# Feed-forward products by one level of Strassen's block algorithm, in a two-layer fp32 encoder on one core

## The chip, the core and the metric

The kernel runs as one launch on one core of a Trainium2 chip. The metric is device time in microseconds (us); the time of a version is the median of its runs. The core's engines are TensorE (PE in the profile; its weight loads are PEld), VectorE (DVE), ScalarE (ACT), GpSimd (POOL) and SyncE (SP). In this kernel SP issues all DMAs, in one queue.

## What is computed

One sequence of 1024 tokens of width 1024 goes through two layers. Layer 0 mixes by windowed attention, layer 1 by a gated linear scan (HGRN2); then each has a feed-forward stage and a gated addition of a projected side input p (called PLE in the kernel). All inputs are fp32. Cut to what matters:

```
def swiglu(x, w_in, w_out):            # w_in 1024 x 5632, w_out 2816 x 1024
    gu = x @ w_in
    g, u = jnp.split(gu, 2, axis=-1)
    return (jax.nn.silu(g) * u) @ w_out

for i in range(2):
    mix = windowed_gqa(x, ...) if i == 0 else hgrn2_bidirectional(x, ...)
    x = layer_norm(ALPHA * x + mix, ln_mix_g[i], ln_mix_b[i])
    x = layer_norm(ALPHA * x + swiglu(x, ffn_w_in[i], ffn_w_out[i]), ln_ffn_g[i], ln_ffn_b[i])
    x = x + jax.nn.sigmoid(x @ ple_w_gate[i]) * (p[i] @ ple_w_proj[i])
```

## The kernel before

**Tiles.** Everything is held transposed: 128 features in the partitions, 512 tokens (half of them, h = 0 or 1) in the free dimension. x is 8 such tiles for each half (index k or m), the hidden width 2816 is 22 tiles (index f). Activations live in the pool `acts` of 48 tiles of 128x512 fp32.

**Products.** An fp32 operand is split into a high part, which ScalarE makes by a copy that rounds to the type fp32r, and a low part, which VectorE or GpSimd makes by subtraction (`split`, lines 67 to 69). One product is three matmuls into the same PSUM bank, high by high, high by low and low by high (`mm3`, lines 182 to 185), each 128x128 by 128x512. `lin` is a chain of eight of these over k. Weights come raw from DRAM in tiles of 128x512 or smaller (`load_w`), through three buffers, and are split into five others; a list of all weight tiles in order of use (`plan`) is fetched one entry ahead of the products (`take_w`).

**Feed-forward stage** (`ffn_ple`). The 22 tiles f go in four groups of 5, 5, 6 and 6 (`GROUPS`). For each f and h, `pair` makes g and u (two `lin`, 24 matmuls each), silu and the product on ScalarE and VectorE, and splits the result h into the pool `hp` of 16 tiles. After each group `acc` multiplies its h tiles with `w_out` into one bank for each of 8 output tiles m and each half (fo), and adds the bank to the tile Y[m][h], which stays in `acts`.

**Normalization.** `layer_norm` is a generator that runs beside other products. Means over the features are taken on TensorE with a matrix of 1/1024 (`average`): first the mean (mu), then the sum of squares v of the eight tiles less the mean, its mean (var), square root and reciprocal (rs), then each tile times rs, with gain and bias on ScalarE, and its split into the new x (`new_x`, low parts on GpSimd).

**Order.** `weave(main, side, ratio)` advances a side generator by `ratio` steps for each step of the main one; the order of calls is the order of priority, from which a scheduler makes the order on each engine. In the feed-forward stage:

```
weave(first(0), pend, 0.65)
drain(first(1))
...
drain(last(0))
weave(last(1), norms[0], 0.9)
weave(ple(0), norms[1], 0.7)
```

`pend` is the normalization of the second half behind the mixer. Beside it stand the products of the first group for the first half (`first(0)`), which read only the first half of x. The output products of the last group go half by half (`last`), so that the normalization of the first half, `norms[0]`, stands beside those of the second, and `norms[1]` beside the PLE products of the first half.

## Time and profile before

| | |
|---|---|
| median of 3 runs | 2974.35 us (2973.11 to 2977.14) |
| span of the profiled execution | 2974.4 us |
| TensorE busy | 2846.8 us, 96% |
| VectorE, ScalarE, GpSimd busy | 58%, 37%, 23% |
| DMA | 197.22 MB, mean 66 GB/s |
| feed-forward matmuls | 6336 of 13584 |

The profile is one execution on the chip. "Busy" is the time in which at least one instruction of an engine runs; matmuls are pipelined and overlap, so the mean duration of one is not what it costs. Windows of the trace count instructions by their start. PEclk is the clock that TensorE was granted, as a share of full speed.

### The profile page before, as it was taken

The page shows a single profiled execution, that of the slowest core. Times are in us where ns is not written, and L with a number is a line of the kernel's source. Part 1 is how long each engine was busy: PE and PEld are TensorE (multiplying, and loading weights), DVE is VectorE, ACT ScalarE, POOL GpSimd, SP SyncE. Part 2 cuts the span into 40 slices and gives each one's busy share as a digit, 9 for nine tenths or more (in the row PEclk, how much of TensorE's full clock was granted, in tenths as well). Part 3 has the DMA queues.
Part 4 walks back from the last instruction along what each step waited for, and adds up shares of the span by engine and source line. Part 5 has one row for each costly group of instructions (what it writes and reads, how often), then busy time and mean ns, then how long its engine had stood idle before and what let it go on. Part 6 is the DMA issues. An engine that isn't in the chain of part 4 may idle for free.

```text
span 2974.4 us, 36435 instructions
## 1 busy us (share of the span) xinstructions
PE 2846.8 (96%) x13584; PEld 2319.0 (78%) x13584; DVE 1730.6 (58%) x2797; ACT 1100.1 (37%) x2032; POOL 678.5 (23%) x476
## 2 busy tenths in 40 slices
PE   8989999999999998999998999999999999999989
PEld 6666778888888886787887778778788888888867
DVE  6878886322223237758888887897843232222484
ACT  4555655221121225544444444344531212112362
POOL 4243242000000004653343433422400000000252
PEclk9999999999999999999999999999999999999999
DMA  4111233211111112321111211212221111111223
GB/s 159 48 43 47 68 98 94 61 54 39 57 42 55 46 57 78 100 85 64 58 64 54 65 50 54 67 54 82 86 90 56 38 55 50 45 48 54 75 96 117
DMA packets 117394, 197.22 MB, mean 66 GB/s; under 512 B 13536, under 2 KB 38880, under 8 KB 117216
## 3 DMA queue, kind: packets, MB, share of 16 engines
q1 hardware_dynamic: 117216, 194.88, 21.0%
q8 instruction: 107, 1.75, 0.2%
q14 instruction: 71, 0.58, 0.1%
HBM read 190.64 MB, written 4.19 MB: 66 GB/s over the span
## 4 chain that ended last, share of the span: by engine, by line
PE 76%; DVE 16%; ACT 4%; issue 3%; POOL 1%; DMA 1%; SPq 0%; DVEq 0%; ACTq 0%; POOLq 0%
PE u L185 5%; PE u L183 5%; PE u L184 5%; PE g L183 5%; PE g L184 5%; PE g L185 5%; PE fo L185 5%; PE fo L183 5%; PE fo L184 5%; PE zps L185 2%; PE zps L183 2%; PE zps L184 2%; PE lv L715 2%; PE s L360 2%; PE pgps L185 1%
## 5 line engine op out<-in xcount | busy, mean ns | idle before, releaser
L183 PE MATMUL fo<-h,w_fo 128*128 128x512 f32 x704 | 278.1, 395 | 0.0
L185 PE MATMUL fo<-h,w_fo 128*128 128x512 f32 x704 | 278.1, 395 | 0.0
L184 PE MATMUL fo<-h,w_fo 128*128 128x512 f32 x704 | 278.0, 395 | 0.0
L184 PE MATMUL g<-xl,w_fg 128*128 128x512 f32 x704 | 274.2, 390 | 3.2 <-POOL xl L69 3.1
L512 DVE TENSOR_TENSOR sg<-sg,u 128x512 f32<-128x512 f32 x88 | 60.5, 688 | 370.8 <-PE u L185 369.4
L183 PE MATMUL g<-xh,w_fg 128*128 128x512 f32 x704 | 274.3, 390 | 1.2 <-ACT sg L511 1.2
L185 PE MATMUL u<-xh,w_fu 128*128 128x512 f32 x704 | 274.6, 390 | 0.0
L183 PE MATMUL u<-xh,w_fu 128*128 128x512 f32 x704 | 274.6, 390 | 0.0
L184 PE MATMUL u<-xl,w_fu 128*128 128x512 f32 x704 | 274.4, 390 | 0.0
L185 PE MATMUL g<-xh,w_fg 128*128 128x512 f32 x704 | 274.0, 389 | 0.0
L69 POOL TENSOR_TENSOR w_hz<-r_hz,w_hz 128x512 fp32r<-128x512 f32 x128 | 181.1, 1422 | 330.5 <-ACT w_hz L68 322.9
L183 PE MATMUL zps<-xh_n,w_hz 128*128 128x512 f32 x512 | 213.4, 417 | 0.0
L68 ACT CAST w_fo<-r_fo 128x384 fp32r<-128x384 f32 (+1 forms) x160 | 78.6, 492 | 338.0 <-PE fo L185 276.2
L185 PE MATMUL zps<-xh_n,w_hz 128*128 128x512 f32 x512 | 203.6, 398 | 0.0
L184 PE MATMUL zps<-xl_n,w_hz 128*128 128x512 f32 x512 | 202.0, 394 | 0.0
L69 DVE TENSOR_TENSOR w_fu<-r_fu,w_fu 128x512 fp32r<-128x512 f32 x108 | 79.9, 742 | 161.4 <-ACT w_fu L68 161.4
L69 DVE TENSOR_TENSOR w_fo<-r_fo,w_fo 128x384 fp32r<-128x384 f32 (+1 forms) x160 | 88.3, 552 | 120.5 <-ACT w_fo L68 120.5
L185 PEld LDWEIGHTS fo<-h,w_fo 128*128 128x128 f32 x704 | 131.9, 187 | 32.3
L184 PEld LDWEIGHTS g<-xl,w_fg 128*128 128x128 f32 x704 | 132.3, 188 | 31.9 <-POOL xl L69 4.5
L184 PEld LDWEIGHTS fo<-h,w_fo 128*128 128x128 f32 x704 | 131.9, 187 | 32.3
L183 PEld LDWEIGHTS fo<-h,w_fo 128*128 128x128 f32 x704 | 132.0, 187 | 32.1
L222 POOL TENSOR_TENSOR s<-hy,hy 128x512 f32<-128x512 f32 x4 | 5.8, 1450 | 658.9 <-DVE hy L531 613.4
(291 smaller groups left out, 6836.2 us busy)
## 6 DMA issues: line engine op xcount, KB each, us to landing
r_hz<-in_whg_dram SPq DMA_DIRECT2D x128, 256.0 KB, 2.6
r_fg<-in_wfi_dram SPq DMA_DIRECT2D x108, 256.0 KB, 2.6
r_fu<-in_wfi_dram SPq DMA_DIRECT2D x108, 256.0 KB, 2.7
r_fo<-in_wfo_dram SPq DMA_DIRECT2D x128, 192.0 KB, 2.3
r_pg<-in_wpg_dram SPq DMA_DIRECT2D x64, 256.0 KB, 2.8
r_qkv<-in_wqkv_dram SPq DMA_DIRECT2D x40, 256.0 KB, 2.7
r_ao<-in_watt_o_dram SPq DMA_DIRECT2D x32, 256.0 KB, 2.7
r_hv<-in_wvh_dram SPq DMA_DIRECT2D x32, 256.0 KB, 3.0
```

The lines of the kernel that those rows point to most:

```text
L68: act.copy(hi, src)
L69: (eng or dve).tensor_tensor(lo, src, f32(hi), op=ALU.subtract)
L183: pe.matmul(ps, lhsT=w[0], rhs=x[0], start=start, stop=False)
L184: pe.matmul(ps, lhsT=w[0], rhs=x[1], start=False, stop=False)
L185: pe.matmul(ps, lhsT=w[1], rhs=x[0], start=False, stop=stop)
L222: (eng or dve).tensor_tensor(s, yprev, y, op=ALU.add)
L360: pe.matmul(sp[r][:, :n * P], lhsT=qq[rs], rhs=kk[rs], start=i == 0, stop=i == 2)
L512: dve.tensor_tensor(sg, sg, u, op=ALU.mult)
L715: pe.matmul(lv[:, c], lhsT=ks[:, c * P:(c + 1) * P], rhs=view(Qq, c * P, dims), start=True, stop=True)
```

## The change

The feed-forward products of both layers are made by one level of the Winograd form of Strassen's algorithm: a product of 2x2 blocks by seven block products of sums and differences, where before there were eight.

- **Input side.** The blocks of x are the feature halves (k 0 to 3 and 4 to 7) by the token halves; those of the weights are the two halves of the features for g and for u. For each f there are seven products p of four `mm3` (`times`): 1 and 2 read x of the first half as it is, 6, 5, 7 and 4 read the sums t2, t1, t3, t4 of x, and 3 reads x of the second half. Weight sums are made on GpSimd (in `head`, `both`, `mid_tail` of the plan), three or four for each f, and g and u come out by additions on VectorE. The order is 1 and 2 of f (`head`), 4 and 3 of f - 1 (`tail`), 6, 5 and 7 of f (`mid`).
- **Sums of x.** `layer_norm` of the second half behind the mixer now takes the tiles in the order 0, 4, 1, 5, ... and calls `combine` after every second one, which makes t1 to t4 (two on VectorE, two on GpSimd) and splits them and the second half of x, the four sums into the pool `hp` (tile `xc`).
- **What stands beside that normalization.** `all_early`: products 1 and 2 of the first four f (`NA`), in place of the first group's products for the first half; the ratio is 2.
- **DRAM.** `combine` stores the 16 tiles Y in DRAM. The h tiles are combined for pairs of f (`spill`, four differences on GpSimd for each pair) and the seven tiles of a pair are stored in DRAM; so are the sums of `w_out` (`w_sums`, four on GpSimd for each pair). One layer stores 77 + 44 + 16 tiles of 256 KB.
- **Output side** (`matmuls_out`). Blocks are the parity of f in a pair (11 pairs), the halves of the output features and of the tokens. It loads the 16 Y again, then runs seven products one after the other in the order 1, 2, 6, 7, 4, 5, 3, each of 11 steps; a step loads one tile of weights and one of h, splits both and runs 12 matmuls, into four banks. The low part of weights is made by GpSimd (VectorE for product 7), that of h by VectorE. After product 4 the first half is complete, and its normalization is woven beside products 5 and 3.
- **Weights** are fetched up to four entries ahead (three on the output side), and loads of three entries are begun ahead of their splits; raw tiles lie in `acts`. `w_out` is laid out by rows on the host.

The diff, cut to its core:

```diff
-GROUPS = [(0, 5), (5, 10), (10, 16), (16, 22)]
+AHEAD = 4
+NA = 4
+ORDER = [1, 2, 6, 7, 4, 5, 3]
...
+        def combine(Y, k):
+            a, b, c, d = Y[k][0], Y[k][1], Y[k + KH][0], Y[k + KH][1]
...
+            dve.tensor_tensor(t1, b, a, op=ALU.subtract)
+            dve.tensor_tensor(t2, d, t1, op=ALU.subtract)
+            pool.tensor_tensor(t3, d, b, op=ALU.subtract)
+            pool.tensor_tensor(t4, c, t2, op=ALU.subtract)
+            fx["x"][6].append(keep(t2, dve))
+            fx["x"][5].append(keep(t1, dve))
+            fx["x"][7].append(keep(t3, dve))
+            yield
+            fx["x"][4].append(keep(t4, pool))
+            hi, lo = A("xh22", F32R), A("xl22", F32R)
+            split(hi, lo, d, dve)
+            fx["x"][3].append((hi, lo))
+            for m in (k, k + KH):
+                for h in range(2):
+                    sync.dma_start(fx["y"][m, h], Y[m][h])
...
-            for m in range(KT):
+            mixed = which == 0 and h == 1
+            for m in [m + i for m in range(KH) for i in (0, KH)] if mixed else range(KT):
                 dve.tensor_tensor(ys[m], ys[m], rs, op=ALU.mult)
...
+                elif m >= KH:
+                    yield from combine(Y, m - KH)
...
+                def times(ps, f, p, start):
+                    w = take_w("w", f, p, ahead=AHEAD)
+                    for k in range(KH):
+                        mm3(ps, w[k], xs[p][k], start and k == 0, k == KH - 1, True)
...
+                def spill(k, sa, sb):
+                    (a, b), (c, d) = sa["h"], sb["h"]
+                    t3, t2, t4 = A("th3"), A("th2"), A("th4")
+                    pool.tensor_tensor(t3, d, b, op=ALU.subtract)
+                    pool.tensor_tensor(b, b, a, op=ALU.subtract)
+                    pool.tensor_tensor(t2, d, b, op=ALU.subtract)
+                    pool.tensor_tensor(t4, c, t2, op=ALU.subtract)
...
+                def matmuls_in():
+                    sts = {}
+                    for f in range(FT):
+                        st = sts[f] = {}
+                        if f >= NA:
+                            yield from head(f, st)
+                        if f:
+                            yield from tail(f - 1, sts[f - 1])
+                        store()
+                        yield from mid(f, st)
+                        if f % 2 == 0 and f:
+                            spill(f // 2 - 1, sts.pop(f - 2), sts.pop(f - 1))
+                        elif f % 2:
+                            w_sums(f // 2)
...
+                def matmuls_out():
...
+                            sync.dma_start(Y[m][h], fx["y"][m, h])
...
+                    for p in ORDER:
...
+                        for k in range(FP):
+                            w, hh = take_w("o", p, k, ahead=AHEAD - 1)
+                            for i in range(4):
+                                mm3(into[i], w[i], hh, p in (1, 2, 5) and k == 0, k == FP - 1, True)
...
-                weave(first(0), pend, 0.65)
-                drain(first(1))
...
-                weave(last(1), norms[0], 0.9)
+                weave(all_early(), pend, 2)
+                drain(matmuls_in())
+                out = matmuls_out()
+                while next(out) != "half":
+                    pass
+                weave(out, norms[0], 0.9)
                 weave(ple(0), norms[1], 0.7)
```

In two places the prediction rests on the order on an engine. The first is the start of the stage of layer 0. On TensorE before, where the output projection of attention (aops) is followed by the products of the first f:

```order
L184 MATMUL aops<-ql_2099,w_ao_4_4248 128x512
L185 MATMUL aops<-qh_2098,w_ao_4_4248 128x512
L183 MATMUL g<-xh_4215,w_fg_0_4300 128x512
L184 MATMUL g<-xl_4216,w_fg_0_4300 128x512
L185 MATMUL g<-xh_4215,w_fg_0_4300 128x512
```

TensorE after, where product 2 of the fourth early f (za) ends; xc are the split sums of x, and the first bank x behind za is product 6 of f 0:

```order
L318 MATMUL za<-xh_4348,w_4627 128x512
L319 MATMUL za<-xl_4349,w_4627 128x512
L320 MATMUL za<-xh_4348,w_4627 128x512
L318 MATMUL x<-xc,wp_4679 128x512
L319 MATMUL x<-xc,wp_4679 128x512
L320 MATMUL x<-xc,wp_4679 128x512
L318 MATMUL x<-xc,wp_4679 128x512
L319 MATMUL x<-xc,wp_4679 128x512
L320 MATMUL x<-xc,wp_4679 128x512
L318 MATMUL zy<-xc,wp_4729 128x512
```

Between the last product that reads only the first half of x and the first that reads a sum stand no other matmuls. VectorE before, from the reciprocal of the second half's normalization on (w_fg, w_fu are split weights, sg the gated product):

```order
L254 RECIPROCAL rs<-rs 128x256 x2
L512 TENSOR_TENSOR sg<-sg,u 128x512
L257 TENSOR_TENSOR y_3982<-y_3982,rs 128x512
L69 TENSOR_TENSOR w_fu_0_4648<-r_fu_0_4646,w_fu_0_4648 128x512
L69 TENSOR_TENSOR h_4643<-sg,h_4643 128x512
L69 TENSOR_TENSOR w_fu_4_4653<-r_fu_4_4651,w_fu_4_4653 128x512
L69 TENSOR_TENSOR w_fg_0_4658<-r_fg_0_4656,w_fg_0_4658 128x512
L257 TENSOR_TENSOR y_4038<-y_4038,rs 128x512
```

And after, from the same place (wp are split weights, tx the sums of x):

```order
L415 RECIPROCAL rs<-rs 128x256 x2
L74 TENSOR_TENSOR wp_4843<-wraw,wp_4843 128x512
L419 TENSOR_TENSOR y_3984<-y_3984,rs 128x512
L419 TENSOR_TENSOR y_4187<-y_4187,rs 128x512
L419 TENSOR_TENSOR y_4040<-y_4040,rs 128x512
L376 TENSOR_TENSOR tx_4657<-y_3984,y_2800 128x512
L419 TENSOR_TENSOR y_4239<-y_4239,rs 128x512
L377 TENSOR_TENSOR tx_4658<-y_4187,tx_4657 128x512
L419 TENSOR_TENSOR y_4091<-y_4091,rs 128x512
L696 TENSOR_TENSOR g_4674<-u_4624,za 128x512
L74 TENSOR_TENSOR xc<-tx_4658,xc 128x512
L74 TENSOR_TENSOR xc<-tx_4657,xc 128x512
```

The sums and their splits now stand among the eight multiplies by rs. GpSimd in the same place before:

```order
L224 TENSOR_TENSOR s<-s,y_4294 128x512
L69 TENSOR_TENSOR xl_4336<-y_3903,xh_4335 128x512
L69 TENSOR_TENSOR xl_4348<-y_3942,xh_4347 128x512
L245 TENSOR_TENSOR v<-v,sq 128x512 x4
L69 TENSOR_TENSOR xl_4637<-y_3982,xh_4636 128x512
```

And after (s and wraw are weight sums of the first f):

```order
L74 TENSOR_TENSOR xl_4349<-y_3944,xh_4348 128x512
L359 TENSOR_TENSOR s<-s,y_4300 128x512
L220 TENSOR_TENSOR s_4596<-wraw 128x512
L406 TENSOR_TENSOR v<-v,sq 128x512
L222 TENSOR_TENSOR s_4598<-wraw 128x512
L223 TENSOR_TENSOR wraw<-s_4598,wraw 128x512
L195 TENSOR_TENSOR wraw<-wraw 128x512
L406 TENSOR_TENSOR v<-v,sq 128x512 x3
L378 TENSOR_TENSOR tx_4659<-y_4187,y_3984 128x512
L379 TENSOR_TENSOR tx_4660<-y_3702,tx_4658 128x512
L74 TENSOR_TENSOR xc<-tx_4660,xc 128x512
```

Four weight sums now stand among the additions to v. The second place is where the input side of layer 0 ends, on SP. Before, at the end of the fourth group's output products, only weight loads stand in the queue:

```order
L74 DMA r_fo_0_7626<-in_wfo_dram 128x384
L74 DMA r_fo_3_7631<-in_wfo_dram 128x384
L74 DMA r_fo_0_7676<-in_wfo_dram 128x384
L74 DMA r_fo_3_7681<-in_wfo_dram 128x384
L74 DMA r_fg_0_7726<-in_wfi_dram 128x512
L74 DMA r_fg_4_7731<-in_wfi_dram 128x512
```

After, between the input and the output side (h_10 are the DRAM tiles of the last pair, th its differences; y the tiles Y that come back):

```order
L766 DMA h_10_4445<-h_7939 128x512
L766 DMA h_10_4412<-th_8087 128x512
L766 DMA h_10_4434<-th_8088 128x512
L794 DMA y_8100<-y_4364 128x512
L794 DMA y_8102<-y_4366 128x512
...
L794 DMA y_8114<-y_4378 128x512
L146 DMA wraw<-in_wfo_dram 128x512
L146 DMA wraw<-h_6_4386 128x512
```

The stores of the last pair stand ahead of the 16 loads of Y, and these ahead of the loads of output step 6.

## Rows read from the trace of the kernel before

**Rows 1.** Page, parts 1 and 2: span, engines, bandwidth in 40 slices.
```profile
span 2974.4 us, 36435 instructions
...
PE 2846.8 (96%) x13584; PEld 2319.0 (78%) x13584; DVE 1730.6 (58%) x2797; ACT 1100.1 (37%) x2032; POOL 678.5 (23%) x476
...
GB/s 159 48 43 47 68 98 94 61 54 39 57 42 55 46 57 78 100 85 64 58 64 54 65 50 54 67 54 82 86 90 56 38 55 50 45 48 54 75 96 117
```

**Rows 2.** Page, part 4: chain that ended last, shares by engine.
```profile
PE 76%; DVE 16%; ACT 4%; issue 3%; POOL 1%; DMA 1%; SPq 0%; DVEq 0%; ACTq 0%; POOLq 0%
```

**Rows 3.** Window: length, busy us of PE, PEld, DVE, ACT, POOL, clock, DMA, GB/s.
```profile
500.00:600.00 100.00, 100.00 (x436) 81.47 (x435) 35.29 (x57) 22.33 (x41) 0.00 (x0) 1.00 0.23 70
```

**Rows 4.** Page, part 5; tiles g, fo: ns shortest/median/longest, first and last start.
```profile
L184 PE MATMUL g<-xl,w_fg 128*128 128x512 f32 x704 | 274.2, 390 | 3.2 <-POOL xl L69 3.1
...
L183 PE MATMUL g<-xh,w_fg x704: 388/389/500, 430.5 to 2763.6; 128*128 128x512 f32 x176
...
L185 PE MATMUL fo<-h,w_fo x704: 392/396/397, 545.8 to 2838.1; 128*128 128x512 f32 x176
```

**Rows 5.** Timeline of PE, from u to fo: start, length, instruction.
```profile
1089.10 0.39 PE L183 MATMUL u<-xh,w_fu 128*128 128x512 f32 x1
...
1094.54 0.40 PE L183 MATMUL fo<-h,w_fo 128*128 128x512 f32 x1
...
1098.05 0.40 PE L183 MATMUL fo<-h,w_fo 128*128 128x512 f32 x1
```

**Rows 6.** Groups by line: busy us, mean ns, idle before.
```profile
L69 POOL TENSOR_TENSOR w_hz<-r_hz,w_hz 128x512 fp32r<-128x512 f32 x128 | 181.1, 1422 | 330.5 <-ACT w_hz L68 322.9 <-PE lv L715 4.6 <-issue 2.0
...
L69 DVE TENSOR_TENSOR w_fu<-r_fu,w_fu 128x512 fp32r<-128x512 f32 x108 | 79.9, 742 | 161.4 <-ACT w_fu L68 161.4
...
L68 ACT CAST w_fu<-r_fu 128x512 fp32r<-128x512 f32 x108 | 66.7, 618 | 102.4 <-PE fo L185 37.3 <-PE u L185 36.2 <-issue 21.2
...
L252 ACT ACT_TABLE_LOAD x7 | 9.0, 1283 | 0.1
```

**Rows 7.** Timelines of DVE, then POOL, second half's normalization, layer 0.
```profile
441.67 1.88 DVE L239 TENSOR_TENSOR y<-y,mu 128x512 f32<-128x512 f32 x3 [0.52 <-PE mu L230]
...
456.17 0.69 DVE L69 TENSOR_TENSOR avl<-v,avh 128x512 fp32r<-128x512 f32 x1
...
466.04 3.37 DVE L254 RECIPROCAL rs<-rs 128x256 f32<-128x256 f32 x2 [4.01 <-ACT rs L252]
...
474.06 2.48 DVE L257 TENSOR_TENSOR y<-y,rs 128x512 f32<-128x512 f32 x4
477.07 5.19 DVE L257 TENSOR_TENSOR y<-y,rs 128x512 f32<-128x512 f32 x3
...
454.18 1.30 POOL L245 TENSOR_TENSOR v<-v,sq 128x512 f32<-128x512 f32 x1 [1.29 <-DVE v L245]
...
478.63 6.17 POOL L69 TENSOR_TENSOR xl<-y,xh 128x512 fp32r<-128x512 f32 x4 [0.33 <-ACT xh L68]
```

**Rows 8.** Windows of 4 us, first half's normalization, layer 0; columns of Rows 3.
```profile
1160.00:1164.00 4.00, 4.00 (x18) 2.90 (x16) 4.00 (x5) 2.96 (x5) 4.00 (x3) 1.00 0.33 98
1164.00:1168.00 4.00, 0.03 (x1) 0.00 (x0) 4.00 (x3) 3.28 (x6) 4.00 (x4) 0.92 0.00 0
1168.00:1172.00 4.00, 1.22 (x2) 0.50 (x2) 4.00 (x5) 2.25 (x5) 4.00 (x3) 0.50 0.22 66
1172.00:1176.00 4.00, 2.50 (x6) 2.01 (x7) 4.00 (x5) 1.66 (x4) 2.58 (x2) 0.50 0.21 66
1176.00:1180.00 4.00, 4.00 (x16) 3.18 (x15) 1.37 (x3) 1.90 (x2) 0.00 (x0) 0.80 0.52 163
```

**Rows 9.** Window at the start; DMA issues, page part 6: KB, us to landing.
```profile
10.00:15.00 5.00, 5.00 (x15) 3.97 (x16) 3.95 (x7) 3.88 (x7) 0.94 (x1) 1.00 1.01 372
...
r_fg<-in_wfi_dram SPq DMA_DIRECT2D x108, 256.0 KB, 2.6
...
xraw<-in_xT_dram SPq DMA_DIRECT2D x16, 256.0 KB, 5.8
```

More of the change, by code (lines that the diff above doesn't have):

```diff
@@ L114, in take_w, with pair_of, blocks @@
             assert k == key, (k, key)
-            fetch_w()
-            return w
+            while len(ready) < ahead and at[0] < len(plan) and (not ready or plan[at[0]][3]):
+                fetch_w()
+            return w
+        fx = {}
+        def pair_of(raw, name, eng=None):
+            hl = wp.tile([P, 2, HALF], F32R, tag="hl", bufs=5, name=name)
+            split(hl[:, 0], hl[:, 1], raw, eng)
+            return hl[:, 0], hl[:, 1]
+        def blocks(hl):
+            return [(hl[0][:, k * P:(k + 1) * P], hl[1][:, k * P:(k + 1) * P]) for k in range(4)]
@@ L525, in acc @@
                         if k % 2:
                             yield
-                    y = Y[m][h]
-                    if gi == 0:
-                        dve.scalar_tensor_tensor(y, y, ALPHA, ps, ALU.mult, ALU.add)
-                    else:
-                        dve.tensor_tensor(y, y, ps, op=ALU.add)
-                    if st is not None:
-                        sum_in(st, y, m, Y[m - 1][h], pool)
-                def first(h):
-                    for f in range(*GROUPS[0]):
-                        yield from pair(f, [h], *w_in(f))
@@ L539, in last, with early @@
-                def last(h):
-                    gi = len(GROUPS) - 1
-                    f0, f1 = GROUPS[gi]
-                    s = T("to", "s")
-                    for m in range(KT):
-                        yield from acc(gi, m, h, take_w("fo", m), s)
-                    norms[h] = layer_norm([Y[m][h] for m in range(KT)], s, li, 1, X, h)
+                def early(f):
+                    x = bank("xa")
+                    yield from times(x, f, 1, True)
+                    u1 = u1s[f] = A("u1")
+                    act.copy(u1, x)
+                    z = bank("za")
+                    yield from times(z, f, 2, True)
+                    g0s[f] = g0 = A("g0")
+                    dve.tensor_tensor(g0, u1, z, op=ALU.add)
+                    act.activation(g0, g0, AF.Silu)
@@ new lines, in head, with mid, out @@
+                def head(f, st):
+                    x = st["x"] = bank("x")
+                    yield from times(x, f, 1, True)
+                    u1 = T("t0", "u1")
+                    act.copy(u1, x)
+                    z = MM("z")
+                    yield from times(z, f, 2, True)
+                    g0 = st["g0"] = A("g0")
+                    dve.tensor_tensor(g0, u1, z, op=ALU.add)
+                def mid(f, st):
+                    u1 = u1s.get(f)
+                    x = st["x"] = bank("x") if u1 is not None else st["x"]
+                    yield from times(x, f, 6, u1 is not None)
+                    u2 = st["u2"] = T("t1", "u2")
+                    def out(t):
+                        if u1 is None:
+                            act.copy(t, x)
+                        else:
+                            dve.tensor_tensor(t, u1, x, op=ALU.add)
+                    out(u2)
+                    z = st["z"] = bank("zy")
+                    yield from times(z, f, 5, True)
+                    yield from times(x, f, 7, False)
+                    u3 = st["u3"] = T("t2", "u3")
+                    out(u3)
+                    dve.tensor_tensor(u3, u3, z, op=ALU.add)
@@ new lines, in w_sums, with store @@
+                def w_sums(k):
+                    e, o = wfo[li][2 * k], wfo[li][2 * k + 1]
+                    a, b, c, d = get(e[:, :HALF]), get(o[:, :HALF]), get(e[:, HALF:]), get(o[:, HALF:])
+                    s3, s1, s2, s4 = sums(a, b, c, d)
+                    lag.append([(fx["sums"][p, k], t) for p, t in ((7, s3), (5, s1), (6, s2), (3, s4))])
+                def store(n=0):
+                    while len(lag) > n:
+                        for dst, src in lag.pop(0):
+                            sync.dma_start(dst, src)
@@ new lines, in matmuls_in @@
+                def matmuls_in():
+                    sts = {}
+                    for f in range(FT):
+                        st = sts[f] = {}
+                        if f >= NA:
+                            yield from head(f, st)
+                        if f:
+                            yield from tail(f - 1, sts[f - 1])
[5 more added lines that the diff above has]
+                            w_sums(f // 2)
+                    yield from tail(FT - 1, sts[FT - 1])
+                    store()
+                    spill(FP - 1, sts[FT - 2], sts[FT - 1])
+                    store()
```

273 lines of the change are left out of this document (218 added, 55 removed).

## The prediction

> **What bounds the kernel now.** I read the page's first two parts [rows 1], then its chain [rows 2], then a window of 100 us inside a feed-forward stage [rows 3]. TensorE is busy 96% of the span and the chain runs through it for 76%; in the stage that the change rewrites it is busy 100.00 of 100.00 us at full clock, while VectorE has 35 us of work and GpSimd none. So this stage costs what its matmuls cost, and there is room on every other engine. A matmul's mean duration there, 389 to 396 ns [rows 4], is not its cost, since they overlap: 24 of the u matmuls start from 1089.10 on and the fo matmuls follow them at 1094.54, so they stand 0.227 us apart; the first 16 of the fo matmuls start between 1094.54 and 1098.05, 0.234 us apart [rows 5]. The u matmuls read tokens from the pool `acts`, the fo matmuls from `hp`; this is the only difference that I see, and I let the spacing go by the pool. Feed-forward matmuls are 704 in each of nine groups [rows 4], 6336 in all, 3168 a layer: 2112 at 0.227 and 1056 at 0.234 make 726 us of a layer, 1452 us of the span.
>
> All sums below are made against the profiled execution, whose span of 2974.4 us [rows 1] is the median of the runs within 0.1 us.
>
> **Part 1: fewer matmuls.** Seven block products take the place of eight. Per layer the input side goes from 2112 to 22 x 7 x 12 = 1848, the output side from 1056 to 7 x 11 x 12 = 924; 792 fewer in the program, as its order shows on TensorE (12150 rows, then 11358). Of the input products three of seven (1, 2, 3) read `acts` and four `hp`: 792 x 0.227 + 1056 x 0.234 = 426 us; output 924 x 0.234 = 216 us. Together 642, a gain of **84 us a layer**. If all input products ran at 0.227 it would be 91, if all ran at 0.234, 78.
>
> **Part 2: the element work beside them.** Per f the input side has 84 matmuls, 19.4 us. GpSimd gets 8 operations for it (4 weight sums, and half of 8 for a pair of f), VectorE 12, ScalarE 12. By prices of the same shapes [rows 6] that is 8 x 1.42 = 11.4, 12 x 0.74 = 8.9 and 12 x 0.62 = 7.4 us. Each fits alone. VectorE and GpSimd slow each other: three multiplies took 5.19 us (1.73 each) beside four GpSimd operations in 6.17 (1.54 each), where alone they took 0.62 and 1.30 [rows 7]. Pairing all 8 at 1.73 and the other 4 VectorE operations at 0.74 gives 16.8 us, still under 19.4. The output side has 2.8 us for each step of 12 matmuls, with one GpSimd operation, one of VectorE and two of ScalarE: 1.73 at most, and 1.24. So I take the element work of the steady loops at nothing, hidden under the matmuls; what it costs without that cover is a rival below.
>
> **Part 3: transfers.** A step of the output side loads two tiles of 0.262 MB in 2.8 us, 187 GB/s; the input side moves 23 tiles for two f, 155 GB/s. The trace of before never needs so much here, but at its start it moved 372 GB/s over 5 us [rows 9]. I take the steady transfers at nothing too.
>
> **Part 4: the seam into the feed-forward products.** Before, the normalization of the second token half runs beside the first group's products, which want only the first half. Now only products 1 and 2 of four f are free of the second half: 96 matmuls, 21.8 us. Product 6 then wants t2 of all four blocks, which come last out of that normalization. In layer 0 (times of before): first product 430.5 [rows 4]; 3.1 us of waits for its split pieces [rows 4]; 21.8; five or six us for the averages and for products 6 and 5 of f 0. Unhindered TensorE would be through these at 462. The data: the first subtraction of the mean is at 441.67 and the variance was summed when the split of `avl` came at 456.17 [rows 7]. GpSimd now has four weight sums among its four additions to v, but VectorE has fewer splits in its way; I leave it at 456. Then two splits, two matmuls, a table load of 1.28, the root, reciprocals 3.37 [rows 6, 7], some 8 us with hand-overs: 464 (466 to 470 before, where the variance matmul stood later among others). From there VectorE has 32 operations up to the last piece of t2, beside 12 on GpSimd: 12 pairs at 1.73 and 20 at 0.62 make 33; I take 31, since the first ones run before GpSimd starts. So 495, and TensorE loses 495 - 462 = 33 us. After a wait the clock also stays low: after that at 1164 it was granted 0.50 from 1168 to 1176, the lower of its two levels, 1.2 of 2.4 GHz, and it was back at full only after some 4 us of work [rows 8]. I add 2.5 us. **+36 us a layer.** Bounds: 24 if no operation slows another (32 x 0.62 = 20), 42 if hand-overs with ScalarE, which has 30 operations in the same chain, show.
>
> The Trainium skill, page "SBUF — State Buffer", section "SBUF: two separate sides", says that a VectorE operation with two SBUF inputs and a GpSimd operation exclude each other for the whole instruction. By it a pair would cost 1.30 + 0.62 = 1.92 us where the trace shows 1.73, the seam some 2 us more a layer, and the whole 2904 where I say 2900. I keep the trace's price.
>
> **Part 5: the seam between the input and output side.** SP issues everything in order. At the end it must store the last pair's sums before the 16 tiles y come back, and only behind these stand the loads of output step 6; steps 0 to 5 are loaded before. With T as the end of the input products: GpSimd first splits step 5, whose weight buffer is free at T + 1.4 (6 matmuls of step 0 left), done at T + 3.6; its four sums of the pair end at T + 9.3. The 16 tiles are 4.2 MB, 11.3 us at 372 GB/s [rows 9]; step 6 lands at about T + 23 and is split at T + 25. Steps 0 to 5 last until T + 15.4 (66 matmuls). Wait 10, clock 2.5: **+13 us a layer.** Bounds 5 (ring and loads overlap better: landing takes 2.6 us [rows 9]) and 20 (5.8 us, as the loads of the start took).
>
> **Part 6: the seam out of it.** Before, output work for the second half (33 us) did not cover the normalization of the first: in the five windows from 1160 to 1180 the matmuls number 18, 1, 2, 6 and 16 [rows 8], 43 where 20 / 0.234 would be 85: 10 us lost. Now products 5 and 3, 22 steps of 2.8 us, stand beside it, so TensorE has 62 us of other work. GpSimd is the tight one: in the last 18 steps it has 18 splits, 8 splits of new x, 4 additions to v and 6 sums, about 53 us against 50 of matmuls, and splits of weights stand behind those of x, which wait for the normalization. I take 8 us of waits in place of 10: **-2 us a layer** (bounds -10 and +6). The wait for the second half's normalization in the gate product that follows stays as it is.
>
> **Sum.** -84 + 36 + 13 - 2 = -37 us a layer, -74 for two: 2974.4 - 74 = **2900 us**. All low bounds: -91 + 24 + 5 - 10 = -72 a layer, 2830; all high ones: -78 + 42 + 20 + 6 = -10, 2954.
>
> **Rivals.** (a) *The seams cost little*: engines overlap better than I have it, start 24, middle 5, end -8 with -84 give -63 a layer, 2848. For it: much of my seam cost is a chain of hand-overs summed by hand; against it: the order puts all four t2 ahead of product 7 whatever the engines do. (b) *VectorE and GpSimd set the pace of the input products*: if they ran strictly one after the other, an f would take 11.4 + 8.9 = 20.3 us and not 19.4; 0.9 x 22 = 20 us a layer, 2940. For it: each of them alone needs more than half of the 19.4 us, and nothing in the trace of before loads both so; against it: three pairs took 1.73 each, less than one after the other [rows 7]. The Trainium skill, page "SBUF — State Buffer", section "SBUF: two separate sides", states an exclusion that would lead here. (c) *Slower: the output side is paced by its transfers.* It moves 77 x 0.524 + 4.2 = 44.6 MB a layer in the 216 us of its matmuls. At the 117 GB/s that the page's last slice moved [rows 1], it would take 381 us, 165 more a layer: 37 us of gain become 128 of loss, 3230. It turns slower where the side lasts over 216 + 37 = 253 us, that is below 176 GB/s. For it: tiles just written to DRAM and re-read, two loads for every 2.8 us on one queue; against it: 372 GB/s at the start [rows 9], on the same queue with tiles of the same size.
>
> **How the numbers follow.** Two runs of this kernel differ by up to 0.2%, 6 us, so faster means under 2968 and slower over 2980. My forecast has 0.62, (a) 0.16, (b) 0.11, (c) 0.06; 0.05 is left for waits in the steady loops that eat the gain. Faster: 0.62 + 0.16 + 0.08 of (b) = 0.86. Same: 0.02 of (b), 0.02 of the rest: 0.04. Slower: (c) 0.06, 0.01 and 0.03: 0.10. The range from 2835 to 2955 leaves out (c), half of the rest, and the ends of (a) and (b).
>
> **What would show it.** Right: 11% to 12% fewer feed-forward matmuls at a spacing of 0.227 to 0.234; TensorE idle for about 33 us at some 25 us after each first product 1, with product 6 waiting for VectorE's split of `xc`; about 10 us idle after output step 5, waiting for weights or h that wait for a DMA; the wait of 8 us at 1164 gone. Wrong: waits of TensorE spread over each f (then (b)), or in each output step with the DMA share near full (then (c)); no wait at the two seams (then (a)).

## The result and the profile after

The changed kernel takes **2907.04 us** (median of 4 runs, 2905.88 to 2908.54), the kernel before 2975.74 us beside it: 0.9767 of it, 95% interval 0.9753 to 0.978. That is 69 us or 2.3% less; the prediction said 2900, 74 less, with a range of 2835 to 2955. Of the runs below one execution, of the run with both edits, took 4372 us at a mean granted clock of 0.56; it counts in no ratio.

The page of the changed kernel, to be set against [rows 1, 2]: span, engines, GB/s in 40 slices, and the chain of work that ended last.

```profile
span 2905.2 us, 37125 instructions
...
PE 2707.3 (93%) x12792; PEld 2175.3 (75%) x12792; DVE 2031.5 (70%) x2949; ACT 1278.9 (44%) x2324; POOL 1384.0 (48%) x968
...
GB/s 160 48 44 44 71 129 71 182 152 163 145 160 263 302 73 95 98 85 63 57 64 51 66 55 59 66 48 81 107 141 167 152 152 163 170 342 202 41 108 118
...
PE 67%; DVE 17%; ACT 5%; issue 4%; POOL 4%; DMA 2%; SPq 0%; ACTq 0%; POOLq 0%; DVEq 0%
```

TensorE has 792 matmuls fewer and is busy 139.5 us less, but only 69.2 us of span went: it now idles 198 us where it idled 128. GpSimd's work has doubled.

Where the time went is read stage by stage, from the first starts of tiles (xa is product 1 of the early f, hvps the first product of layer 1's mixer). Two rows of the changed kernel:

```profile
L956 PE MATMUL hvps<-w_hv,xh_n x256: 274/283/375, 1261.1 to 1822.3; 128*128 128x256 f32 x128
...
L318 PE MATMUL xa<-xh,w x16: 389/389/395, 2070.1 to 2098.4; 128*128 128x512 f32 x16
```

| stage | before | after | difference |
|---|---|---|---|
| up to the first feed-forward product | 430.5 | 429.3 | -1.2 |
| feed-forward and PLE, layer 0 | 862.8 | 831.8 | -31.0 |
| mixer of layer 1 | 811.9 | 809.0 | -2.9 |
| feed-forward and PLE, layer 1 | 869.2 | 835.1 | -34.1 |
| sum | 2974.4 | 2905.2 | -69.2 |

The next rows are windows of layer 0: start of the stage, steady input products, seam between the sides, end of the output side, PLE. Columns: length, busy us of PE with instructions, PEclk, DMA share, GB/s.

```profile
429.20:545.20 116.00, 85.49 (x308) 0.82 0.36 127
545.20:880.20 335.00, 335.00 (x1449) 1.00 0.46 156
...
898.20:960.20 62.00, 49.73 (x202) 0.89 0.88 322
...
1070.20:1142.50 72.30, 67.78 (x278) 0.98 0.22 77
1142.50:1261.10 118.60, 113.95 (x485) 0.97 0.29 93
```

Between the seams TensorE is busy without a gap at full clock. What is lost beside the kernel before stands in the windows at the start and at the seam; the last two windows have gaps as well, as they had before. TensorE's waits in the first window: us in total, times, longest.

```profile
PE x L318 <- ACT xc L73: 19.5, 4, 7.1
PE var L364 <- ACT avh L73: 6.0, 1, 6.0
PE x L318 <- DVE u L719: 2.5, 3, 1.1
```

And in the output side, from 895 to 1110:

```profile
PE ox L318 <- ACT hs L73: 11.8, 1, 11.8
```

x behind za is product 6 and xc a split sum of x; ox is an output product, hs a split tile of h. These are the two waits that the prediction named. The list puts the first one down to ScalarE's casts of the sums, where the prediction had VectorE's splits; the casts themselves wait for VectorE's sums (ScalarE's timeline, block four):

```profile
494.13 1.66 ACT L73 CAST xc<-tx 128x512 fp32r<-128x512 f32 x3 [3.95 <-DVE tx L377]
```

### The profile page after: what moved, and what is told of

Same layout as the page of the kernel before. It is cut to its first block, busy times and chain, and to the rows that moved or that the text cites. A ratio compares the mean times of both kernels' runs of the same rounds, so it can differ in the third digit from the quotient of the medians.

```text
span 2905.2 us, 37125 instructions
## 1 busy us (share of the span) xinstructions
PE 2707.3 (93%) x12792; PEld 2175.3 (75%) x12792; DVE 2031.5 (70%) x2949; ACT 1278.9 (44%) x2324; POOL 1384.0 (48%) x968
## 4 chain that ended last, share of the span: by engine, by line
PE 67%; DVE 17%; ACT 5%; issue 4%; POOL 4%; DMA 2%; SPq 0%; ACTq 0%; POOLq 0%; DVEq 0%
PE x L318 5%; PE x L320 5%; PE x L319 5%; PE zy L318 3%; PE zy L320 3%; PE zy L319 2%; PE ox L319 2%; PE ox L320 2%; PE ox L318 2%; PE zps L320 2%; PE zps L319 2%; PE zps L318 2%; PE lv L1019 2%; PE s L525 2%; PE oz L320 1%
## 5 line engine op out<-in xcount | busy, mean ns | idle before, releaser
L74 POOL TENSOR_TENSOR wo<-wraw,wo 128x512 fp32r<-128x512 f32 x132 | 183.7, 1401 | 230.5 <-ACT wo L73 183.5
L74 DVE TENSOR_TENSOR wp<-wraw,wp 128x512 fp32r<-128x512 f32 x204 | 201.2, 986 | 108.9 <-ACT wp L73 107.9
L74 DVE TENSOR_TENSOR hs<-wraw,hs 128x512 fp32r<-128x512 f32 x154 | 185.0, 1226 | 123.8 <-ACT hs L73 123.6
L318 PE MATMUL x<-xc,wp 128*128 128x512 f32 x528 | 213.4, 405 | 46.4 <-ACT xc L73 41.6
L73 ACT CAST wp<-wraw 128x512 fp32r<-128x512 f32 x204 | 127.0, 622 | 245.0 <-PE zy L320 153.9
L319 PE MATMUL x<-xc,wp 128*128 128x512 f32 x528 | 211.9, 401 | 1.5 <-DVE xc L74 1.5
L320 PE MATMUL x<-xc,wp 128*128 128x512 f32 x528 | 211.1, 400 | 0.0
L73 ACT CAST wo<-wraw 128x512 fp32r<-128x512 f32 x154 | 95.1, 620 | 222.2 <-POOL wo L74 78.7
L318 PE MATMUL ox<-hs,wo 128*128 128x512 f32 x352 | 141.4, 402 | 23.4 <-ACT hs L73 23.4
L318 PEld LDWEIGHTS x<-xc,wp 128*128 128x128 f32 x528 | 100.4, 190 | 79.4 <-ACT xc L73 46.7
L319 PE MATMUL ox<-hs,wo 128*128 128x512 f32 x352 | 141.2, 401 | 1.0 <-DVE hs L74 1.0
L320 PE MATMUL ox<-hs,wo 128*128 128x512 f32 x352 | 140.6, 399 | 0.0
L1019 PEld LDWEIGHTS lv<-Q,ks 128*128 128x128 f32 x768 | 97.8, 191 | 37.0 <-issue 24.3
L1019 PE MATMUL lv<-Q,ks 128*128 128x128 f32 x768 | 105.4, 279 | 20.3 <-DVE tot L1030 10.3
L319 PEld LDWEIGHTS x<-xc,wp 128*128 128x128 f32 x528 | 100.3, 190 | 27.9 <-DVE xc L74 5.2
L320 PEld LDWEIGHTS x<-xc,wp 128*128 128x128 f32 x528 | 100.4, 190 | 24.4
```

The source lines that it names most:

```text
L73: act.copy(hi, src)
L74: (eng or dve).tensor_tensor(lo, src, f32(hi), op=ALU.subtract)
L318: pe.matmul(ps, lhsT=w[0], rhs=x[0], start=start, stop=False, skip_group_check=free)
L319: pe.matmul(ps, lhsT=w[0], rhs=x[1], start=False, stop=False, skip_group_check=free)
L320: pe.matmul(ps, lhsT=w[1], rhs=x[0], start=False, stop=stop, skip_group_check=free)
L1019: pe.matmul(lv[:, c], lhsT=ks[:, c * P:(c + 1) * P], rhs=view(Qq, c * P, dims), start=True, stop=True)
```

## The experiments

Times are medians; where kernels are compared, it is by their ratio to the kernel before on the same chip, in which 0.001 is 3 us and an interval is some 0.0014 to either side. So two runs less than some 0.002 or 6 us apart are not told apart by their times; there the two feed-forward stages of the traces (as in the table, one execution of each run) are set beside them. The changed kernel has 0.9767, and its two stages are 1666.9 us together.

**The order of the sums of x.** Product 6 waits for t2 of all four blocks. The first run makes these first and puts the other sums behind them.

```diff
             dve.tensor_tensor(t2, d, t1, op=ALU.subtract)
-            pool.tensor_tensor(t3, d, b, op=ALU.subtract)
-            pool.tensor_tensor(t4, c, t2, op=ALU.subtract)
             fx["x"][6].append(keep(t2, dve))
+            yield
+            yield "rest"
+            pool.tensor_tensor(t3, d, b, op=ALU.subtract)
+            pool.tensor_tensor(t4, c, t2, op=ALU.subtract)
...
+            for c in rest:
+                yield from c
```

> combine in two passes: t1 and t2 of all four blocks and the splits of t2 first, the rest behind them. Same instructions, other order. Theory (VectorE's row of operations between rs and the last piece of t2 sets the start of product 6): 25 operations stand there in place of 33, which took 33 us in the changed kernel (464.4 to 497.2); with 9 to 12 of them beside GpSimd at 1.73 us and the others at 0.62 the row takes 25 to 29 us, 4 to 8 us less a layer, so 2891 to 2899 against 2907. Rival (hand-overs with ScalarE, which the waits name, set it): the same, 2904 to 2910.

Measured: 2909.78 us, ratio 0.9772 (0.9759 to 0.9785): nothing won. VectorE's timeline in the changed kernel (start, length, operation, count, idle time ahead with its releaser):

```profile
494.78 2.42 DVE L74 TENSOR_TENSOR xc<-tx,xc 128x512 fp32r<-128x512 f32 x3 [0.68 <-ACT xc L73]
```

In this run:

```profile
482.91 1.89 DVE L74 TENSOR_TENSOR xc<-tx,xc 128x512 fp32r<-128x512 f32 x3
...
495.80 1.09 DVE L74 TENSOR_TENSOR xc<-tx,xc 128x512 fp32r<-128x512 f32 x1 [4.26 <-ACT xc L73]
...
502.06 1.09 DVE L74 TENSOR_TENSOR xc<-tx,xc 128x512 fp32r<-128x512 f32 x1 [1.81 <-ACT xc L73]
```

And its waits of TensorE from 425 to 545:

```profile
PE x L318 <- ACT xc L73: 13.7, 4, 6.7
...
PE zy L318 <- ACT xc L73: 1.7, 2, 1.1
PE zy L319 <- DVE xc L74: 1.5, 1, 1.5
```

The first of the three splits at 482.91 and at 494.78 is the last piece of t2. So t2 came 12 us earlier, where the theory of VectorE's row had 4 to 8: GpSimd has 3 operations from 464 to 484 here and 7 in the changed kernel, so fewer of VectorE's stood beside one. But the splits of t1 and t3 now end near 503, behind GpSimd, which makes t3 and t4 among weight sums, and products 5 (zy) and 7 wait for those. Both theories fall in part: the row sets when product 6 can end, but not what the start costs; the rival had the time right, but not by its reason, since t2 did move. What seems to count is when **all** sums of the first f are there; the third run fits that.

**The same sums by another engine.**

```diff
-            pool.tensor_tensor(t3, d, b, op=ALU.subtract)
-            pool.tensor_tensor(t4, c, t2, op=ALU.subtract)
+            dve.tensor_tensor(t3, d, b, op=ALU.subtract)
+            dve.tensor_tensor(t4, c, t2, op=ALU.subtract)
...
-            fx["x"][4].append(keep(t4, pool))
+            fx["x"][4].append(keep(t4, dve))
```

> The sums t3, t4 and the low part of t4 move from GpSimd to VectorE, the order of the blocks stays. The row up to the last piece of t2 has 44 operations in place of 33. Theory of pairs (an operation beside GpSimd costs VectorE 1.73 us, one alone 0.62): with only the weight sums of f 1 left on GpSimd, 4 to 8 pairs, the row takes 32 to 36 us: within 3 us a layer of the changed kernel, 2901 to 2913. Rival (an operation of VectorE costs the 1.0 us that it took on average there, whatever GpSimd does): 44 us, 11 more a layer, 2929.

Measured: 2902.46 us, ratio 0.9748 (0.9735 to 0.9761), 6 us less than the changed kernel, at the edge of what the times tell apart; the two stages of its trace, 1660.9 us, are 6 us less too. A window of VectorE's busiest stretch in this run (columns as in [rows 3]):

```profile
464.00:492.00 28.00, 12.04 (x27) 6.54 (x25) 28.00 (x48) 20.94 (x34) 0.00 (x0) 0.61 0.28 100
```

And in the changed kernel:

```profile
464.00:496.00 32.00, 11.86 (x24) 6.16 (x22) 30.12 (x35) 19.25 (x32) 16.22 (x11) 0.54 0.37 129
```

(The rows of windows count every instruction that overlaps a window and not, as it says ahead of the prediction, those that start in it; by starts VectorE has 46 operations in the first window and 34 in the second.) With GpSimd silent VectorE did 46 operations in 28 us, 0.61 us apart; with 11 operations of GpSimd beside them 34 took 30. The row took 28 us and not the 32 to 36 forecast, as none of GpSimd's weight sums stood beside it: the first came at 494.39. The theory of pairs holds, and the fixed 1.0 us of the rival falls; taking work from GpSimd and giving it to the busier VectorE ended it sooner.

**Both edits.**

> Both edits: t2 of all blocks first, and all sums of x on VectorE. 25 operations up to the last piece of t2, 4 to 8 of them beside weight sums on GpSimd. Theory of pairs: 20 to 24.5 us in place of 33, 8 to 13 us less a layer: 2881 to 2891. Rival (1.0 us each): 25 us, 8 less a layer, but then the splits of t1, t3 and t4 delay products 5, 7 and 4 by some 8 us: 2907. Rival (hand-overs): 2904 to 2910.

Measured: 2900.55 us, ratio 0.9743 (0.973 to 0.9756), some 7 us less than the changed kernel and not told apart from the sums on VectorE alone. That is less than the theory of pairs asked for. The trace kept of it is of the execution of 4372 us, so where the waits stand in it isn't known.

**The 16 tiles Y behind the loads of output step 10.**

```diff
-                    for m0, h in ((0, 0), (0, 1), (KH, 1), (KH, 0)):
-                        for m in range(m0, m0 + KH):
-                            sync.dma_start(Y[m][h], fx["y"][m, h])
...
                             w, hh = take_w("o", p, k, ahead=AHEAD - 1)
+                            if (p, k) == (1, 5):
+                                for m0, h in ((0, 0), (0, 1), (KH, 1), (KH, 0)):
+                                    for m in range(m0, m0 + KH):
+                                        Y[m][h] = A(f"y{m}{h}")
+                                        sync.dma_start(Y[m][h], fx["y"][m, h])
```

> The 16 tiles Y are loaded behind the loads of output step 10 and not ahead of those of step 6; nothing else changes. Theory (the order on SP makes the wait of 11.8 us at the seam between input and output side): step 6 is loaded from 915 on in place of 925, its split ends near 923, TensorE has work until 920: the wait falls to 0 to 3 us and the low clock behind it (2.7 us) mostly goes, 9 to 14 us a layer, 2879 to 2889. Rival (the five buffers of split weights and GpSimd's splits pace the first steps, or the loads, which run at 387 GB/s from 924 on, do): the wait only moves to a later step, 2902 to 2910.

Measured: 2893.35 us, ratio 0.9716 (0.9703 to 0.9729), 15 us less. SP's queue in the changed kernel (start, length, transfers):

```profile
915.13 9.53 SPq L794 DMA_DIRECT2D y<-y  x16
924.99 0.33 SPq L146 DMA_DIRECT2D wraw<-in_wfo_dram  x1
```

In this run:

```profile
916.21 0.37 SPq L146 DMA_DIRECT2D wraw<-in_wfo_dram  x1
...
921.51 12.36 SPq L839 DMA_DIRECT2D y<-y  x16
```

And where TensorE waits in it from the seam on:

```profile
921.99 0.50 PE L319 MATMUL ox<-hs,wo 128*128 128x512 f32 x1 [0.63 <-DVE hs L74]
940.82 2.07 PE L318 MATMUL oz<-hs,wo 128*128 128x512 f32 x4 [4.81 <-ACT hs L73]
```

The wait of 11.8 us is gone, so the order on SP made it. But the block of 16 loads only stands elsewhere: it now holds up the loads of product 2, whose start waits 4.8 us. The time lies between the theory and its rival; the next run parts them.

**Y back by fours**, each behind the loads of the product that first needs it.

```diff
+                    back = {1: (0, 0), 6: (0, 1), 7: (KH, 1), 4: (KH, 0)}
...
+                            if k == 5 and p in back:
+                                m0, h = back[p]
+                                for m in range(m0, m0 + KH):
+                                    Y[m][h] = A(f"y{m}{h}")
+                                    sync.dma_start(Y[m][h], fx["y"][m, h])
```

> The 16 tiles Y come back by fours, each four behind the loads of the last steps of the product that first needs them (1, 6, 7, 4). With all 16 behind the loads of output step 10 the wait of 11.8 us had gone and one of 4.8 us had come at the start of product 2. Theory (any block of loads on SP that is longer than what the steps have loaded ahead makes a wait; 4 tiles take 2.9 us at 387 GB/s): no wait of TensorE over 1 us from the end of the input side to product 4; 5 to 7 us less a layer than with all 16 late, 14 to 15 less than the changed kernel: 2877 to 2883. Rival (loads of steps and the low parts of weights are the limit once the 16 tiles are out of the way): 2890 to 2895.

Measured: 2877.93 us, ratio 0.9673 (0.9659 to 0.9688), 28 us less than the changed kernel, 14 a layer. The seam's window in this run:

```profile
898.20:960.20 62.00, 61.18 (x262) 48.69 (x261) 39.70 (x35) 30.08 (x52) 41.89 (x30) 1.00 0.87 318
```

And its longest wait of TensorE from 890 to 1075:

```profile
PE ox L319 <- DVE hs L74: 0.7, 1, 0.7
```

262 matmuls stand where 202 stood, with the DMA engines as loaded as before (0.87 and 318 GB/s). It was the place of the 16 loads in the order (their buffers are taken later with them); transfers, GpSimd's splits and the five weight buffers aren't the limit.

**Six early f** (`NA = 6`).

> Six early f in place of four (NA = 6): products 1 and 2 of f 4 and 5 move ahead of the first product that reads a sum. Theory (TensorE idles at the start of the stage because its row of ready products, 22 us, is shorter than the normalization and the row of sums on VectorE, which don't move): 48 matmuls, 11 us, move under the idle time; VectorE gets 6 operations more ahead of the row, most in its idle time: 7 to 11 us less a layer, 2885 to 2893. Rival (the element work of all sums sets the pace whatever TensorE has ready, and the added splits delay it; the first run pointed there, since t2 came 13 us earlier and nothing was won): 2902 to 2912.

Measured: 2901.94 us, ratio 0.9747 (0.9733 to 0.9762), 6 us less by its time and 10 by its two stages (1656.5), where the theory's lower end was 14. The waits of TensorE moved to the early products (425 to 560), and ScalarE's timeline shows why:

```profile
PE za L318 <- ACT u L692: 15.7, 2, 10.8
PE xa L318 <- DVE g L696: 7.9, 2, 6.7
```

```profile
490.86 0.62 ACT L73 CAST wp<-wraw 128x512 fp32r<-128x512 f32 x1 [6.09 <-POOL wraw L223]
...
494.43 1.66 ACT L73 CAST xc<-tx 128x512 fp32r<-128x512 f32 x3 [1.39 <-DVE tx L377]
495.99 0.58 ACT L692 COPY u<-xa 128x512 f32<-128x512 f32 x1
```

The copy u and the addition g read the banks of the early products. They stand in ScalarE's and VectorE's rows behind the splits of the sums, and the copy at 495.99 behind a split that waited for GpSimd's weight sum. So more ready products help only as far as the two engines that make the sums also empty the banks.

Nor did the rest stand still, as the theory had it. VectorE's reciprocal in the changed kernel, then in this run:

```profile
461.14 3.36 DVE L415 RECIPROCAL rs<-rs 128x256 f32<-128x256 f32 x2 [2.64 <-ACT rs L413]
```

```profile
456.34 3.37 DVE L415 RECIPROCAL rs<-rs 128x256 f32<-128x256 f32 x2 [1.31 <-ACT rs L413]
```

Counted from the first product (429.3 and 431.1) it begins 6.6 us earlier, since GpSimd's weight sums no longer stand among its additions to v. They stand among the sums of x in their place, from 486 to 492, and the split of the last piece of t2 begins 65.5 us behind the first product in both. The run thus has two changes in it, and what the early products alone are worth is not shown.

**How much element work is free.** On the input side, from f 4 on, the low parts of the weights by GpSimd; then one operation of each f more.

```diff
-                    return blocks(pair_of(st["r"][0], "wp1"))
+                    return blocks(pair_of(st["r"][0], "wp1", pool if f >= NA else None))
...
-                    dve.tensor_tensor(h1, h1, u3, op=ALU.mult)
+                    (pool if f >= NA else dve).tensor_tensor(h1, h1, u3, op=ALU.mult)
```

(The first line so for all seven products; the second only in the second of the two runs.)

> On the input side, from f 4 on, the low parts of the seven weight tiles of an f are made by GpSimd in place of VectorE. Theory of the prediction's part 2 (element work costs nothing while each engine's sum stays under the 19.4 us of an f's matmuls): GpSimd now has some 15 operations for each f, 21 us at 1.42 and 23 at 1.54, so it sets the pace: 2 to 4 us for each of 18 f, 34 to 67 us more a layer, 2975 to 3041. Rival (the buffers and the order let TensorE run ahead of GpSimd, or VectorE, freed of the contention, gives the time back): 2900 to 2930.

> As the run in which GpSimd makes the low parts of the input side's weights from f 4 on, and one operation more of each f goes to GpSimd: the product of silu and u for the second half (h1). In that run GpSimd was busy 98.8% (77 operations of 1.29 us in 100 us) and nothing was lost, so 15 operations of 1.29 us just fit the 19.4 us of an f's matmuls. Theory (an engine's element work is free up to the matmuls' time and then costs what is over): 16 x 1.29 = 20.7 us, 1.3 us over in each of 18 f, 23 us more a layer: 2945 to 2965. Rival (work off TensorE's path stays hidden by buffers): 2904 to 2912.

Measured: 2906.41 us, ratio 0.9764 (0.9747 to 0.978), no change; then 2932.38 us, 0.985 (0.9837 to 0.9864), 24 us more than the changed kernel. Steady windows of the first and of the second run:

```profile
620.00:720.00 100.00, 100.00 (x434) 81.05 (x433) 18.69 (x25) 36.35 (x62) 98.81 (x77) 1.00 0.43 149
```

```profile
620.00:720.00 100.00, 97.83 (x422) 78.71 (x421) 13.76 (x20) 35.35 (x60) 99.22 (x80) 1.00 0.43 148
720.00:820.00 100.00, 96.00 (x413) 76.93 (x412) 13.75 (x20) 34.71 (x60) 99.21 (x81) 1.00 0.44 150
```

An engine at 98.8% of TensorE's time cost nothing; with one operation more for each f, the sixteenth, it set the pace. My number for the first run failed by its price, 1.42 us and more, where 77 operations filled 98.81 us; the 1.30 of one that ran alone [rows 7] was nearer. By starts GpSimd made 159 operations in the second run's 200 us, 1.26 each, and TensorE 832 matmuls where it had made 864: an f takes 20.2 us in place of 19.4, 0.75 more in each of 18 f, 13 a layer, as its two stages have it (13.3 and 13.0 more than the changed kernel's). I had 23, by 1.29 for each operation. The rule holds, with the price of operations that follow each other without a gap.

**Edits together.**

> Three edits at once: six early f, all sums of x on VectorE, Y back by fours. If the seams are separate, the gains add: 7 to 11 and 3 a layer at the start, 14 at the seam between the sides: 24 to 28 a layer, 2851 to 2859. If the start is set by the sum of the element work (rival of the run with six early f): 3 and 14 a layer, 2873.

> Two edits of the three that ran together at 2861.5: all sums of x on VectorE and Y back by fours, but four early f. Alone they gave 6 and 28 us; as separate seams they add: 2873 (2869 to 2877). The six early f gave 6 alone, so the three together would have made 2867; if the two give 2873, the early f bring some 11 us once VectorE makes the sums, since GpSimd then no longer slows the operations that free the banks of the early products. If the two give 2867 or less, the seams help each other and the early f stay at 6.

> The three edits (six early f, sums of x on VectorE, Y back by fours) and the fourth: t2 of all four blocks first. Alone the fourth gave nothing, since the wait went from product 6 to products 5 and 7, whose sums GpSimd made late; with VectorE making them and more early products the sums behind t2 are ready 10 us after it: 2 to 5 us less a layer than the three, 2851 to 2858. Rival (with six early f the waits stand at the early products themselves, for banks that the row of sums keeps from being freed, so the order of sums does nothing): 2859 to 2865.

> The three edits that ran at 2861.5 and, in the normalization ahead of the feed-forward stage, the four additions to v that GpSimd makes (1.3 us each, with hand-overs to VectorE on both sides: 443.8 to 452.7 in that run) made by VectorE too (0.6 us each). Theory (the start of the stage is a chain from the mean over v and rs to the sums, and every hand-over to GpSimd in it lengthens it): rs comes 3 to 5 us earlier, all behind it too, 2851 to 2857. Rival (the chain is paced by ScalarE's squares and by VectorE's other splits, and the early products wait for banks, not for rs): 2858 to 2865.

Measured: three edits 2861.53 us (0.9616, 0.9601 to 0.963); two edits 2871.98 (0.9651, 0.9638 to 0.9664); with t2 first 2866.07 (0.9629, 0.9616 to 0.9642); with the additions to v on VectorE 2864.82 (0.9623, 0.961 to 0.9636). The two add to within 1 us (28 and 6 alone, 34 together), so the seams are separate. The six early f, worth 6 alone, bring 10 on top of them by the times; by the two stages it is 10 alone and 8.5 on top (1619.9 us with three edits, 1628.4 with two), so that they bring more together is not shown. The last two bring nothing. In the last, from the mean on VectorE's operations stand back to back and the reciprocal begins at 456.25, 26.0 us after the first product, where it began at 455.37 with three edits, 25.8 after it. So with six early f the row of v is VectorE's own and not one of hand-overs; of the changed kernel, where weight sums stand among the additions to v and it begins 31.9 us after the first product, this run says nothing. The version with three edits beats both kernels: 114 us less than before, 45 less than the changed one.

## Why the prediction was right

**The matmuls (part 1) held.** Counted by starts, 1447 matmuls stand in the 335.00 us of the input side's steady window, 0.2315 us each, and 214 in the 50 us of the output side from 950 on, 0.2336. That makes 428 and 216 us a layer, where I had 426 and 216. Before, the first window here is the start of the stage, the second the steady products (columns as in [rows 3]):

```profile
430.50:545.30 114.80, 110.70 (x485) 90.56 (x484) 68.42 (x87) 55.17 (x91) 25.31 (x18) 1.00 0.31 97
545.30:1094.50 549.20, 549.20 (x2401) 450.34 (x2400) 149.34 (x232) 105.05 (x184) 0.00 (x0) 1.00 0.16 49
```

2400 start in the second, 0.2288 us each, so 3168 were worth 725 us. The gain is 82; I had 84. (792 of 6336 matmuls are 12.5%, where the prediction's sign has 11% to 12%.) That the spacing goes by the pool is true in part: from 545 to 896 the products that read sums stand 0.2335 us apart and product 2 0.227, but products 1 and 3, which read `acts` too and each follow a product on sums, 0.230.

**Element work and transfers (parts 2 and 3) held.** In the input side's steady windows no wait of TensorE is listed, and in the output side it is busy 4.00 of 4.00 us while the DMA engines are full. The slice from 948 to 952 of the changed kernel:

```profile
948.00:952.00 4.00, 4.00 (x19) 3.21 (x18) 4.00 (x6) 1.25 (x3) 1.74 (x2) 1.00 1.06 387
```

Rival (c) wanted the output side below 176 GB/s; it can have 387. Rival (b) wanted VectorE and GpSimd to set the pace; in the steady windows they are busy 52 and 61 of 100 us. Where GpSimd's own limit lies the runs with work moved show: seven operations more for each f cost nothing, the eighth did.

**The start of the stage (part 4) was sized too small, and its mechanism is only half of it.** In the window of 116 us 307 matmuls start, worth 71.1 at 0.2315, so 44.9 us are lost, and 43.1 in layer 1; the kernel before lost 4.3 and 4.5 in the like windows. That is 41 and 39 us a layer, near the upper bound of 42, where I took 36. The step to the last piece of t2 was right to half a microsecond: forecast 495, measured 494.78 for its start. In part that is luck: the split of avl, forecast at 456, came at 457.8, GpSimd's weight sums standing among the additions to v, and what follows it up to the reciprocals' end at 464.5 took 6.7 us and not 8. What was off is the other side, TensorE's: its products began 1.2 us earlier and waited 1.3 us for their pieces and not 3.1, so by the same sum it would have been through its products 3 us sooner, and it lost 3 us more; that is most of the 5 us in layer 0, and the rest is open. Of the 44.9 us TensorE is idle for 30.5; the others are matmuls at the lower clock, many of them between waits for the sums. The clock stayed at 0.50 in each window of 4 us from 468 to 500 (the last two are shown here) and was back at full by 504:

```profile
492.00:496.00 4.00, 1.20 (x2) 0.57 (x2) 3.28 (x4) 1.87 (x4) 2.10 (x2) 0.50 0.73 243
496.00:500.00 4.00, 4.00 (x10) 2.71 (x10) 1.89 (x3) 1.31 (x3) 3.13 (x3) 0.50 0.05 19
500.00:504.00 4.00, 3.22 (x13) 2.28 (x12) 1.57 (x3) 1.66 (x3) 3.84 (x4) 0.90 0.00 0
504.00:508.00 4.00, 4.00 (x19) 3.25 (x18) 4.00 (x4) 1.15 (x2) 3.92 (x3) 1.00 0.01 4
```

From 496 to 504 20 matmuls start, worth 4.6 us, in 7.2 us of busy time, so 2.6 of these 8 us are the clock, beside 2.5 forecast, and 0.8 waits. And that "product 6 waits for t2" is true of the wait, but the runs showed that t2 is not what the stage pays for: 12 us earlier, it left the time as it was.

**The seam between the sides (part 5) held, each step to some 2 us.** The input products end at T = 903.9. I had TensorE run dry at T + 15.4, step 6 split at T + 25, a wait of 10 and 2.5 for the clock. It ran dry at 919.9 (T + 16.0), the split came at 930.4 (T + 26.5), the wait is 11.8, and in 62 us 200 matmuls start, worth 46.7 at 0.2336, 15.3 lost in all beside 13. Y by fours gave back 14.

**The end of the output side (part 6) held.** 276 matmuls that start in 72.3 us leave 7.8 us lost, and the PLE stage is 11.5 us shorter than before, since the wait after 1164 [rows 8] is gone: -3.7 us, beside -2. GpSimd is the tight engine there, as forecast: it is busy for all of the 20 us from 1110 on, where TensorE waits 3.0 us for VectorE's split of an h tile, 1.1 for GpSimd's low parts of weights, and has the clock at 0.93 and then 0.90. (In [rows 8] 38 matmuls start in the five windows, and not 43, so the kernel before lost 11 us there where the prediction had 10.)

**The sum.** -82 + 41 + 15 - 4 is -30 in layer 0 (measured -31.0) and -82 + 39 + 15 - 4 = -32 in layer 1 (-34.1), beside -37; 1 to 2 us a layer are not accounted for. The layers fall 6 and 3 us short of the forecast, most of it by part 4. The stages that the change doesn't touch are 4 us shorter, for which I had nothing: the mixer of layer 1 took 809.0 us where it had taken 811.9, but in the traces of the other runs, whose mixer is the same, it takes 808.5 to 812.4, so this much changes from execution to execution. That brought the whole to 5 us from the forecast and not 9: luck.

## What to carry to other kernels

When matmuls are saved by sums of operands, the saving came here as counted (82 us a layer for 84) and the cost stood at the seams: list there what the first product needs, on which queue it stands and behind what. Order on an in-order queue is the cheapest repair: splitting one block of 16 loads into four, each where it is needed, gave 28 us, while bringing one operand forward gave nothing, as the others of the same step were still late. Element work beside matmuls was free here up to 98.8% of the matmuls' own time on one engine, so count it per step for each engine, with the price it has under load.

## What was not expected of the hardware

**GpSimd's operations cost VectorE more than moving the work to VectorE does.** In the changed kernel 34 operations of VectorE took 30.1 us beside 11 of GpSimd; at 0.61 each they would have taken 21, so each GpSimd operation held VectorE up for some 0.8 us, while the same operation on VectorE costs 0.6. With GpSimd busy all the time the operations of VectorE that read a bank keep 0.69 us, and the one that reads two tiles takes 1.67, where it took 0.69 in the changed kernel, with GpSimd busy 61% (first run with GpSimd's low parts, 620 to 820: count, busy us, mean ns):

```profile
L745 DVE TENSOR_TENSOR h<-h,u 128x512 f32<-128x512 f32 x10 | 16.7, 1670 | 7.0 <-ACT h L744 7.0
L727 DVE TENSOR_TENSOR u<-u,zy 128x512 f32<-128x512 f32 x11 | 7.6, 689 | 65.1 <-ACT u L717 65.1
```

The Trainium skill, page "SBUF — State Buffer", section "SBUF: two separate sides", says that a VectorE operation with two SBUF inputs and a GpSimd operation that reads SBUF share a pair of ports as an exclusive lock, which the one that starts first holds for the whole instruction while the other blocks, and that on the engines' side only this pair of ports causes contention. These two rows agree with it.
